# Channel-major weight units: both 512-column products of a k tile ahead of both 256-column ones

## The chip, the cores and the metric

The kernel runs on one NeuronCore of a Trainium2 chip. The metric is the device time of one execution in microseconds, the median of several runs; less is better.

## What is computed

One decoder layer over 256 tokens of width 2048, all in float32. It is a SwiGLU feed-forward half step, then token mixing of two branches side by side (a gated sparse attention of 16 heads and an mLSTM of 4 heads), merged through gates, then a second SwiGLU half step:

```python
def rms_norm(x, gain):
    y = x32 * lax.rsqrt(jnp.mean(x32 * x32, axis=-1, keepdims=True) + EPS)
    return (y * gain).astype(x.dtype)

def swiglu(x, w_gate, w_up, w_down):
    return (jax.nn.silu(x @ w_gate) * (x @ w_up)) @ w_down

x = x + 0.5 * swiglu(rms_norm(x, ffn1_norm), ffn1_w_gate, ffn1_w_up, ffn1_w_down)
hn = rms_norm(x, mix_norm)
proj = hn @ w_in + b_in            # queries, keys, values, gates
...
merged = gates_a * (o_nsa @ w_branch_nsa) + gates_b * (h_m @ w_branch_mlstm)
x = x + merged @ w_out
x = x + 0.5 * swiglu(rms_norm(x, ffn2_norm), ffn2_w_gate, ffn2_w_up, ffn2_w_down)
```

The feed-forward width is 5632. Nearly all of the arithmetic is in the products with the weight matrices, about 408 MB of float32 that are read once.

## The kernel before

Every large product is made in the reduced float32 form of the tensor engine (float32r) from split operands. An activation a is kept as two float32r parts, high and low, side by side: XX, H, M_, O_ and h_ have the shape [128, k tiles, 2, 256 tokens], the index of size 2 being the part. A weight block w is split as it arrives: ACT writes the high part whi as a cast copy of the raw tile (split_hi), DVE writes the low part wlo as the difference (split_lo). The product is then hi·hi + hi·lo + lo·hi.

**The weight stream.** A Unit is a block of a weight matrix that goes through the tensor engine tile by tile. Each tile has 1024 elements per partition (512 KB), is loaded by one DMA on the SP queue into one of 4 raw buffers, and is split into one of 4 whi and one of 4 wlo buffers. The list `plan` holds all tiles in order; the loop at the end of the kernel walks it, and emits the products of each tile in two halves (e = 0 and 1). Between the halves it may start a step of side work (small products of the norms, the attention and the mLSTM), and it issues the split of the tile three places ahead.

There are three kinds of units:

- unit_a, channel-major: the weights are stationary, and the output is [128 columns of w, tokens]. A unit covers 256 columns of w, so a tile holds four k tiles of 128 rows. For each k tile and each block c of 128 columns there are two products: whi against both parts of the activation, 512 columns that move, into the PSUM bank ps[:, c, 0:512], and wlo against the high part alone, 256 columns that move, added into ps[:, c, 0:256]. The function fold adds the two halves of the bank afterwards. All units of the two feed-forward steps are of this kind (but for the last one), and so are the q/k projections of the mLSTM, the merge gates, the two branch outputs and w_out. One narrow unit (w_small, 128 columns) has a single block c.
- unit_b, token-major: the activations are stationary, and the weights move, always 512 columns. Eight or so projections of the mixing stage are of this kind.
- unit_last: the last unit of the second feed-forward step, with three products of 256 columns for each k tile and block.

A guest unit (cmp_unit, the hidden layer of the key and value compression, 256 columns that move) is put between the tiles of a token-major unit. Each product has a weight load of its own ahead of it in the tensor engine's queue. The function mul emits a product of the stream, and behind it a few of the small side products that are waiting, if any (deque small_ones). The class Estimate keeps rough times by which side work is placed; it sums over products, so it is the same for any order of the same products.

In the trace all instructions have the line of one helper, L110, so they are told apart by the tiles: mm<-XX,whi is a product of a channel-major unit with the high part of the weights, mm<-XX,wlo one with the low part, mm<-whi,XX one of a token-major unit.

Of the kernel before, what the change touches and what calls it, by code (L numbers as in the profile page):

```python
# [31 lines left out]

# columns of the packed per-partition vectors
C_G1, C_GM, C_G2 = 0, 16, 32
# [11 lines left out]
class Unit:  # L46
    """A weight matrix block that runs through the tensor engine, tile by tile."""

# [5 lines left out]
class Estimate:  # L54
    """Rough times (us) at which the engines get through what they've been given so far, to tell when a
    piece of side work can go into the tensor engine's queue without holding it up."""
    TABLES = {AF.Exp: 1, AF.Silu: 2, AF.Sigmoid: 3, AF.Gelu_apprx_tanh: 4, AF.Ln: 5}
# [5 lines left out]
    def after(self, t):  # L63
        """What follows on the other engines depends on t, and in turn on itself."""
        self.at, self.by, self.end = t, None, t
# [30 lines left out]
class Engine:  # L96
    """Passes calls on, and counts them in the estimate; or keeps them for later (in kept)."""

# [16 lines left out]
def layer(ctx: ExitStack, tc: tile.TileContext, xt, cols, w_small, b_in,  # L115
# [22 lines left out]
    def side_bank(tag):  # L138
        """A bank for side work; free: the times its two banks are given back."""
        est.q["T"] = max(est.q["T"], free[tag].pop(0))  # L140
        held.append(tag)
        free[tag].append(1e9)
        return aux.tile([128, 512], F32, name=nm(tag), tag=tag, bufs=2)
# [4 lines left out]

    # ------------------------------------------------------------------ persistent tiles
    cl = per.tile([128, NCOL], F32, name="cl")  # L150
# [18 lines left out]

    # ------------------------------------------------------------------ helpers  # L170
    def rsqrt(o, ss, n, inv):
        """o = 1/sqrt(ss*inv + EPS), by Newton steps."""
        v = small(n, tag="rv", bufs=2)[0:o.shape[0]]
        t = small(n, tag="rt", bufs=2)[0:o.shape[0]]
        V.tensor_scalar(v, ss, inv, EPS, op0=OP.mult, op1=OP.add)
        V.tensor_scalar(t.bitcast(I32), v.bitcast(I32), 1, None, op0=OP.logical_shift_right)
        V.tensor_scalar(o.bitcast(I32), t.bitcast(I32), -1.0, float(0x5F3759DF), op0=OP.mult, op1=OP.add)
        for _ in range(3):
            V.scalar_tensor_tensor(t, o, -0.5, o, op0=OP.mult, op1=OP.mult)
            V.tensor_mul(t, t, v)  # L180
            V.scalar_tensor_tensor(o, t, 1.5, o, op0=OP.add, op1=OP.mult)

    cur = {}

    # Side work goes in jobs, and these in steps: products first (up to a yield), then what takes
    # them up (up to a yield, of the names of the jobs that have to be over before it goes on, or of the
    # time from which on it can).
    jobs, past = [], {}
# [27 lines left out]
    def step(forced=None):  # L216
        """Starts a step of a job, if one is due; those without products are done at once."""
        while jobs:
# [30 lines left out]
    def mul(*a, **k):  # L249
        """A product of the weight stream; some small ones of the side work go in behind it."""  # L250
        T.matmul(*a, **k)
        for _ in range(min(len(small_ones), 2 + len(small_ones) % 2)):
            small_ones.popleft()()

    def settle():
        """Takes up the small products that were spread over the last ones of the weight stream."""
        while small_ones:
            small_ones.popleft()()
        j, cur["late"] = cur.get("late"), None
        if j:  # L260
            uptake(j)
# [16 lines left out]

    # ------------------------------------------------------------------ weight stream
    tiles = []  # L280
# [54 lines left out]
    def blocks(w, c0, ncol, kts):  # L335
        """The tiles [128, nk, ncol] of 1024 elements per partition of w[:, c0:c0+ncol]."""
        nk = 1024 // ncol
        v = w.rearrange("(k p) n -> p k n", p=128)
        return [(v[:, k:k + nk, c0:c0 + ncol], nk, ncol) for k in range(0, kts, nk)]

    def unit_b(w, c0, H, L, kts, done, pre=None):
        """Token-major: out[tok, 512 columns], activations stationary."""
        def emit(ps, h, e, wh, wl):
# [9 lines left out]
    def unit_a(w, c0, ncol, kts, act, done, pre=None):  # L353
        """Channel-major: out[128 columns, tok] for each 128 of ncol columns, weights stationary."""
        nk = 1024 // ncol

        def emit(ps, h, e, wh, wl):
            a = act()
            for k in range(e * nk // 2, (e + 1) * nk // 2):
                kt = nk * h + k  # L360
                for c in range(ncol // 128):
                    cs = slice(c * 128, c * 128 + 128)
                    mul(ps[:, c, :], wh[:, k, cs], a[:, kt].rearrange("p a t -> p (a t)"), start=kt == 0, stop=False)
                    mul(ps[:, c, 0:S], wl[:, k, cs], a[:, kt, 0, :], start=False, stop=kt == kts - 1)
        return Unit(blocks(w, c0, ncol, kts), emit, done, pre)

    def unit_last(w, c0, ncol, kts, act, done):
        """As unit_a, but with one sum, and one 128 columns after the other at the end; done(ps, c) for each."""
        nk = 1024 // ncol
# [18 lines left out]
    def fold(o, ps, c=2):  # L388
        """Sum of the two halves that unit_a leaves."""
        A.copy(o, ps[:, 0:c, S:])  # L390
# [3 lines left out]

    # ------------------------------------------------------------------ residual stream pieces

    def g_r():
        """rstd of the residual: R per token, and RB along the free axis on each partition."""
        ps = psS()
# [17 lines left out]
    def residual(pool, c, ps, half, gcol, name):  # L417
        """Adds 256 channels to X; then scales and splits them for the next products."""
        y = pool.tile([128, 2, S], F32, name=nm("y"), tag="y", bufs=2)
# [32 lines left out]

    # ------------------------------------------------------------------ FFN
    def ffn(wg, wu, wd, first, nxt, name):
        """first: the job that leaves this norm's rstd; nxt: the next norm's gain column, or None for
        the last one (then it is stored); name: the job that leaves the next rstd."""
        env = {}
# [61 lines left out]

    # ------------------------------------------------------------------ mixing  # L520
    def mixing():
# [50 lines left out]

        # ---- gate tile: rows 0-3 forget, 32-35 input, 64-111 attention gates
        def gate_done(ps):
# [44 lines left out]

        # ---- compressed keys and values  # L620
        def kcvc_done(ps):
# [6 lines left out]
        def g_flat(kc, w):  # L628
            """The blocks' positions on the partitions, split; columns (part, group, block)."""
            tr = psT().rearrange("p (g t) -> p g t", g=2)  # L630
# [9 lines left out]
            for lp in range(2):  # L640
                o = slice(lp * 64, lp * 64 + 64)
                for gpar in range(2):
                    v = tr[gpar * 64:gpar * 64 + 64, :, lp:]
                    # token 16 * block + 2 * k + lp of group 2 * g + gpar
                    src = bass.AP(tensor=v.tensor, offset=v.offset, ap=[v.ap[0], [2, 16], [S, 2], [16, 15]])
# [70 lines left out]

        # ---- queries and keys, normalised
        def normed(src, dst, n):
            """src, dst [128, 2, 64*n/2]: each 64 columns divided by their rms."""
            yield  # L720
# [39 lines left out]
        def g_qt(q, g):  # L760
            """Of each head of the group, both parts of its queries, one below the other."""
            qs = env["q", g] = env["N"].tile([128, 4, S], F32R, name=nm("qs"), tag="qs", bufs=2)
# [15 lines left out]
        def g_kk(g):  # L778
            """The keys of the group (selected, window), split, each part on both halves of the partitions."""
            kk = env["k", g] = env["N"].tile([128, 2, 2, S], F32R, name=nm("kk"), tag="kk", bufs=2)  # L780
# [23 lines left out]

        # ---- attention
        def gates_of(g):
            """Attention gates of the group: [tok, tile, head, branch]."""
            return env["gat"].rearrange("p t (g r b) -> p t g r b", g=4, r=4)[:, :, g]
# [131 lines left out]

        # ---- mLSTM
        def mv_done(c):
# [149 lines left out]

        # ---- merge
        def sig_done(key, c):
# [103 lines left out]

    # ------------------------------------------------------------------ start
    nc.scalar.dma_start(cl, cols)  # L1200
# [55 lines left out]

    # ------------------------------------------------------------------ run
    banks = {}
# [87 lines left out]
```

## Time and profile before

| | |
|---|---|
| median of 3 runs | 2255.24 us (2254.92 to 2256.05) |
| span of the profiled execution, first to last instruction | 2240.6 us |
| what lies around the span (median less span) | 14.6 us |
| PE busy | 2228.4 us, 99% |
| DVE, ACT busy | 1370.9 us (61%), 1105.6 us (49%) |
| HBM read | 408.40 MB, 183 GB/s over the span |

The span is that of one execution under the profiler; the timed runs are others, and the profiled one has no time of its own but its span. PE is TensorE's products, PEld its weight loads, which overlap the products. The end of a product is modelled by the profiler and overlaps the start of the next; the starts are what is measured. The stages, roughly: the first feed-forward step until 740 us, the token-major projections and the attention until 1020 us, the mLSTM projections and the merge until 1500 us, then the second feed-forward step.

### The profile page before, as it was taken

Reading aid. Unit: us, or ns where it says so; the run is one execution under the profiler, and the core shown is the slowest. Engines: PE = TensorE matmul, PEld = TensorE weight load, DVE = VectorE, ACT = ScalarE, POOL = GpSimd, SP = SyncE. Lnnn points to the kernel's source line nnn. Section 1 sums busy time; section 2 is a strip of 40 time slices with the busy share of each in tenths; the row PEclk is TensorE's granted clock in tenths of the full one; section 3 lists DMA queues with packets and bytes.
Section 4 is the critical chain, followed back from the end, with each engine's and each line's share of the span. In section 5 each row is a group of like instructions: output and inputs, shape, how many; then the busy total and the mean of one; then the engine's idle time right before and its main releaser. Section 6 shows DMA issues by size and latency. Waiting matters only on the chain.

```text
span 2240.6 us, 31889 instructions
## 1 busy us (share of the span) xinstructions
PE 2228.4 (99%) x12685; PEld 1928.6 (86%) x12685; DVE 1370.9 (61%) x1711; ACT 1105.6 (49%) x1471; POOL 27.8 (1%) x54
## 2 busy tenths in 40 slices
PE   9999999999999999999999999999999999999999
PEld 7888888888888888778888888888888888888888
DVE  7656555555555677776766666665555555554553
ACT  6444444444444455566775544554444444443332
POOL 0000000000000000001100000000000000000000
PEclk9999999999999999999999999999999999999999
DMA  7666666666555676444556666655665556565663
GB/s 246 189 190 191 191 188 189 188 188 198 188 189 189 185 238 187 148 123 130 152 163 192 186 187 185 194 182 185 187 186 185 185 185 187 185 195 193 196 196 124
DMA packets 395078, 412.59 MB, mean 184 GB/s; under 512 B 13296, under 2 KB 375920, under 8 KB 394928
## 3 DMA queue, kind: packets, MB, share of 16 engines
q1 hardware_dynamic: 394064, 408.08, 58.9%
q0 software_dynamic: 720, 2.36, 0.4%
q8 instruction: 99, 1.62, 0.3%
q14 instruction: 51, 0.42, 0.1%
q10 hardware_dynamic: 144, 0.11, 0.0%
HBM read 408.40 MB, written 2.10 MB: 183 GB/s over the span
## 4 chain that ended last, share of the span: by engine, by line
PE 97%; DVE 1%; ACT 1%; DMA 1%; issue 0%; SPq 0%; DVEq 0%; ACTq 0%
PE mm L110 94%; PE sc L110 2%; PE tr L110 2%; DVE wlo L110 0%; DMA X<-in_xt_dram 0%; DMA raw<-in_w_in_dram 0%; DVE t L110 0%; DVE nx L110 0%; ACT whi L110 0%; ACT kk L110 0%; ACT t L110 0%; DVE y L110 0%; DVE kk L110 0%; ACT qs L110 0%; ACT XX L110 0%
## 5 line engine op out<-in xcount | busy, mean ns | idle before, releaser
L110 DVE TENSOR_TENSOR wlo<-raw,whi 128x1024 fp32r<-128x1024 f32 (+1 forms) x772 | 929.4, 1224 | 583.4 <-ACT whi L110 580.6
L110 PE MATMUL mm<-XX,whi 128*128 128x512 f32 x3600 | 1269.4, 397 | 4.8 <-DVE XX L110 4.8
L110 ACT CAST whi<-raw 128x1024 fp32r<-128x1024 f32 (+1 forms) x772 | 793.6, 1046 | 581.1 <-PE mm L110 450.1
L110 PE MATMUL mm<-XX,wlo 128*128 128x256 f32 x3600 | 1011.5, 281 | 0.9 <-DVE wlo L110 0.8
L110 PEld LDWEIGHTS mm<-XX,whi 128*128 128x128 f32 x3600 | 676.2, 188 | 165.0 <-ACT whi L110 5.8
L110 PEld LDWEIGHTS mm<-XX,wlo 128*128 128x128 f32 x3600 | 681.2, 189 | 2.7 <-DVE wlo L110 2.5
L110 PE MATMUL mm<-H,whi 128*128 128x512 f32 (+1 forms) x1496 | 493.6, 382 | 0.5 <-DVE y L110 0.5
L110 PE MATMUL mm<-H,wlo 128*128 128x256 f32 x1408 | 395.0, 281 | 0.0
L110 PEld LDWEIGHTS mm<-H,whi 128*128 128x128 f32 x1496 | 274.5, 188 | 58.6 <-DVE y L110 0.7
L110 PEld LDWEIGHTS mm<-H,wlo 128*128 128x128 f32 x1408 | 266.0, 189 | 0.0
L110 PE MATMUL mm<-whi,XX 128*128 128x512 f32 x576 | 192.3, 400 | 0.0
L110 PEld LDWEIGHTS mm<-whi,XX 128*128 128x128 f32 x576 | 108.2, 188 | 21.5 <-issue 0.7
L110 PE MATMUL mm<-wlo,XX 128*128 128x512 f32 x288 | 113.8, 395 | 0.2 <-DVE wlo L110 0.2
L110 PE MATMUL mm<-M__10731,whi 128*128 128x512 f32 x256 | 90.5, 397 | 0.0
L110 PE MATMUL mm<-M__10731,wlo 128*128 128x256 f32 x256 | 71.9, 281 | 0.0
L110 ACT COPY sg<-mm 128x512 f32<-128x512 f32 x44 | 25.8, 587 | 79.8 <-PE mm L110 79.8
L110 ACT COPY sh<-mm 128x512 f32<-128x512 f32 x44 | 25.8, 587 | 78.4 <-PE mm L110 78.4
L110 PEld LDWEIGHTS mm<-wlo,XX 128*128 128x128 f32 x288 | 54.3, 188 | 9.9 <-DVE wlo L110 0.6
L110 DVE TENSOR_TENSOR sg<-mm,sg 128x512 f32<-128x512 f32 x44 | 30.4, 692 | 50.6 <-ACT sg L110 50.5
L110 DVE TENSOR_TENSOR sh<-mm,sh 128x512 f32<-128x512 f32 x44 | 30.4, 692 | 50.2 <-ACT sh L110 50.2
L110 PEld LDWEIGHTS mm<-M__10731,whi 128*128 128x128 f32 x256 | 48.1, 188 | 11.9
L110 ACT CAST H<-sh 128x512 fp32r<-128x512 f32 x44 | 27.3, 621 | 62.1 <-DVE sh L110 62.1
(192 smaller groups left out, 1221.1 us busy)
## 6 DMA issues: line engine op xcount, KB each, us to landing
raw<-in_wu_dram SPq DMA_DIRECT2D x176, 512.0 KB, 4.7
raw<-in_wd_dram SPq DMA_DIRECT2D x176, 512.0 KB, 4.5
raw<-in_wg_dram SPq DMA_DIRECT2D x175, 512.0 KB, 4.7
raw<-in_w_in_dram SPq DMA_DIRECT2D x168, 512.0 KB, 4.4
raw<-in_w_out_dram SPq DMA_DIRECT2D x32, 512.0 KB, 4.5
raw<-in_wb_n_dram SPq DMA_DIRECT2D x16, 512.0 KB, 5.1
raw<-in_wb_m_dram SPq DMA_DIRECT2D x16, 512.0 KB, 4.4
bias<-in_b_in_dram POOLq DMA_DIRECT2D x9, 256.0 KB, 3.7
```

What stands on the lines that cost most here:

```text
L110: return g(out, *a, **k)
```

## The change

In the function emit of unit_a the loop over the blocks c is split in two: first the 512-column products of all blocks of the k tile, then the 256-column products of all blocks. For a unit of 256 columns the order within a k tile becomes whi block 0, whi block 1, wlo block 0, wlo block 1, where it was whi block 0, wlo block 0, whi block 1, wlo block 1. The rest of the diff removes comments and docstrings.

```diff
         def emit(ps, h, e, wh, wl):
             a = act()
             for k in range(e * nk // 2, (e + 1) * nk // 2):
                 kt = nk * h + k
                 for c in range(ncol // 128):
                     cs = slice(c * 128, c * 128 + 128)
                     mul(ps[:, c, :], wh[:, k, cs], a[:, kt].rearrange("p a t -> p (a t)"), start=kt == 0, stop=False)
+                for c in range(ncol // 128):
+                    cs = slice(c * 128, c * 128 + 128)
                     mul(ps[:, c, 0:S], wl[:, k, cs], a[:, kt, 0, :], start=False, stop=kt == kts - 1)
         return Unit(blocks(w, c0, ncol, kts), emit, done, pre)
```

## Rows read from the trace of the kernel before

**Rows 1.** The page's head and the busy time of each engine.

```profile
span 2240.6 us, 31889 instructions
...
PE 2228.4 (99%) x12685; PEld 1928.6 (86%) x12685; DVE 1370.9 (61%) x1711; ACT 1105.6 (49%) x1471; POOL 27.8 (1%) x54
```

**Rows 2.** Groups of PE's products by operands: busy us, mean ns | idle before.

```profile
L110 PE MATMUL mm<-XX,whi 128*128 128x512 f32 x3600 | 1269.4, 397 | 4.8 <-DVE XX L110 4.8
L110 PE MATMUL mm<-XX,wlo 128*128 128x256 f32 x3600 | 1011.5, 281 | 0.9 <-DVE wlo L110 0.8
...
L110 PE MATMUL mm<-H,wlo 128*128 128x256 f32 x1408 | 395.0, 281 | 0.0
...
L110 PE MATMUL mm<-M__10731,wlo 128*128 128x256 f32 x256 | 71.9, 281 | 0.0
...
L110 PE MATMUL mm<-h__9138,wlo 128*128 128x256 f32 x128 | 36.0, 281 | 0.0
L110 PE MATMUL mm<-O__6437,wlo 128*128 128x256 f32 x128 | 36.0, 281 | 0.0
```

**Rows 3.** Busy time of each engine by stretch, then clock and DMA.

```profile
core 0: us, PE busy (x) PEld busy (x) DVE busy (x) ACT busy (x) POOL busy (x), PEclk, DMA share, GB/s
...
14.00:44.00 30.00, 29.87 (x172) 25.77 (x170) 24.19 (x31) 21.47 (x32) 0.00 (x0) 1.00 0.82 262
45.00:740.00 695.00, 695.00 (x4013) 612.87 (x4012) 402.68 (x411) 319.40 (x365) 0.00 (x0) 1.00 0.61 190
...
1020.00:1183.00 163.00, 162.51 (x942) 141.70 (x938) 113.23 (x214) 114.21 (x174) 16.56 (x21) 1.00 0.54 158
1183.00:2205.00 1022.00, 1022.00 (x5795) 886.87 (x5794) 596.30 (x614) 470.32 (x550) 0.00 (x0) 1.00 0.61 189
```

**Rows 4.** Timeline of PE in FFN1: start us, busy us, product.

```profile
300.30 0.39 PE L110 MATMUL mm<-XX,whi 128*128 128x512 f32 x1
300.53 0.28 PE L110 MATMUL mm<-XX,wlo 128*128 128x256 f32 x1
300.65 0.39 PE L110 MATMUL mm<-XX,whi 128*128 128x512 f32 x1
```

**Rows 5.** Timeline of the weight loads in the same stretch.

```profile
300.30 0.19 PEld L110 LDWEIGHTS mm<-XX,wlo 128*128 128x128 f32 x1
300.53 0.19 PEld L110 LDWEIGHTS mm<-XX,whi 128*128 128x128 f32 x1
```

**Rows 6.** Timeline of PE in FFN2.

```profile
2000.05 0.40 PE L110 MATMUL mm<-H,whi 128*128 128x512 f32 x1
2000.29 0.28 PE L110 MATMUL mm<-H,wlo 128*128 128x256 f32 x1
2000.40 0.40 PE L110 MATMUL mm<-H,whi 128*128 128x512 f32 x1
...
2001.11 0.40 PE L110 MATMUL mm<-H,whi 128*128 128x512 f32 x1
```

**Rows 7.** Timeline of PE in a token-major unit; nine products lie between these starts.

```profile
799.71 0.39 PE L110 MATMUL mm<-wlo,XX 128*128 128x512 f32 x1
...
801.75 0.39 PE L110 MATMUL mm<-wlo,XX 128*128 128x512 f32 x1
```

**Rows 8.** Timeline of PE at the guest block's start and end (16 products).

```profile
803.56 0.28 PE L110 MATMUL sc<-whi,flat 128*128 128x256 f32 x1
803.67 0.28 PE L110 MATMUL sc<-wlo,flat 128*128 128x256 f32 x1
...
805.47 0.40 PE L110 MATMUL mm<-whi,XX 128*128 128x512 f32 x1
805.71 0.40 PE L110 MATMUL mm<-wlo,XX 128*128 128x512 f32 x1
805.94 0.62 PE L110 MATMUL mm<-whi,XX 128*128 128x512 f32 x2
```

**Rows 9.** Timeline of PE: small side products within the stream of FFN1.

```profile
43.90 0.50 PE L110 MATMUL sc<-ones,acc 128*128 128x2 f32 x4
```

## The prediction

> **What bounds the kernel now.** I read the page first. The span is 2240.6 us and PE is busy for 99% of it [rows 1], so no other engine can matter except by making PE wait. The groups of products by operand come next: the pairs of the channel-major units (a 512-column product with whi, a 256-column one with wlo) are 3600 + 1408 + 256 + 128 + 128 products of 256 columns, less 88 of unit_last, so 5432 pairs; PE idles 4.8 us ahead of the 512s, once, at the start, and 0.9 us ahead of the 256s [rows 2]. Nothing is waited for in the body. What is left to change is the pace at which products follow each other, and a busy time can't show that, because the products overlap in it (0.39 us busy, the next one 0.23 us later [rows 4]). So I went to starts.
>
> The table of stretches is the first thing to look at [rows 3]: the granted clock is 1.00 in all of them, PE has no gap, and yet the paces differ. From 45 to 740 us, 4013 products in 695 us make 2005 pairs at 0.347 us. From 1183 to 2205 us, 5795 products, all but 12 in pairs, make 2891 pairs at 0.3535 us. The timeline of single products says the same: 300.30 to 300.65 is 0.35 for one pair, split 0.23 and 0.12 [rows 4]; and 2000.05 to 2001.11 is 1.06 for three pairs, 0.3533 each [rows 6]. So the same code runs at two paces, A (346.7 ns) and B (353.3 ns), 6.7 ns apart. B is not FFN2's own: the first 44 us of FFN1 have it too, and there it ends right behind a group of small side products at 43.90 [rows 9]. I take the pace for a state in which the stream settles after a disturbance and which it then keeps. In B the 256 still takes 0.11 to 0.12 us (2000.29 to 2000.40); the 6.7 ns lie on the 512 (0.24 at 2000.05) [rows 6].
>
> How much there is to win: pairs at B are some 2891 after 1183 us, some 95 in the first 45 us, and about half of the 416 between 1020 and 1183 us, where side work keeps disturbing it (my choice; that half is worth 1.4 us) [rows 3]. That is some 3190 pairs x 6.67 ns = 21.3 us above pace A, 0.9% of the time.
>
> **The change part by part.** Per k tile of 256 columns the order 512, 256, 512, 256 becomes 512, 512, 256, 256. No instruction is added or removed; the 16 pairs of the gate unit (128 columns, one block) keep their order, so 5416 pairs are 2708 k tiles that change. DMAs, splits, folds and PSUM banks are the same.
>
> *What moves for the other engines.* wlo is first read one 512-product later, 0.23 us: that can win at most the 0.9 us of idle time ahead of wlo products [rows 2]; I take 0.3. The last read of a whi tile starts one 256-product (0.12 us) sooner, which hands the buffer back to ACT sooner; PE doesn't wait for ACT anywhere in [rows 2], so it is worth 0; without the cover of the four buffers it would be a gain too. The last product of a unit is the same one, so the folds start as before. Side products that follow each product of the stream now stand behind other products, in the same number.
>
> *What moves on PE: the sequence of sizes.* Each product has its own weight load, which starts with the product before it: loads start at 300.30 and 300.53, as the products do, and show 0.19 us [rows 5]. Before, each k tile had two loads beside 512s and two beside 256s; after, also two and two. So a load finds as much cover as before, only in another order. The new neighbours are 512 behind 512 and 256 behind 256. The trace has both. In the token-major units, 512s alone: 799.71 to 801.75 is 2.04 for nine products, 227 ns each [rows 7]. 256s alone, in the guest block of the compression unit: 803.67 to 805.47 is 1.80 for fifteen, 120 ns each [rows 8]. Two of each are 693 ns, which is pace A again (2 x 346.7). So equal neighbours cost nothing over A, and A cannot be beaten by them: that is the lower bound, 693 ns for a k tile, against 707 in B.
>
> What the crossing from one size to the other costs is shown at the ends of the same block. The first 256 behind the 512s takes 0.11 (803.56 to 803.67), the first 512 behind the 256s 0.24 (805.47 to 805.71) and the second 0.23 [rows 8]. With a second 256 at 0.12 that is 0.24 + 0.23 + 0.11 + 0.12 = 0.70 us for one round trip of two and two, 7 ns over the 693. B has the same 7 ns for a round trip of one and one. So the reading I choose: the 6.67 ns of B are paid once per round trip from 256 to 512 and back, and the change halves the round trips. In A they are not paid, and 693 stays 693.
>
> The sum, with states as they are now: 3190 pairs are 1595 k tiles; one price in place of two saves 1595 x 6.67 ns = 10.6 us. With the 0.3 us for wlo, 10.9 us. The 14.6 us between span and median (2255.24) are untouched. 2255.24 - 10.9 = 2244.3 us, or -0.48%; the profiled execution's span would go from 2240.6 to 2229.7. Bounds: all k tiles at 693 saves the 21.3 us; all at 707 (the price paid twice in each) adds 6.67 ns x the 5432 - 3190 = 2242 pairs now at A, 15.0 us; the 0.70 us read at the block's ends, taken for every k tile, is 350 ns a pair against a mean of 346.7 + 21.3 us / 5432 = 350.6 now, next to no change.
>
> *A rule against a row.* The row: a 512 that another 512 follows takes 227 ns, a 256 that a 256 follows 120 ns, each some 13 ns over its columns at 2.4 GHz [rows 7, 8]. The Trainium skill (TensorE: Matmul & The Clock Gate, Back-to-back issue gap) gives a product's distance to the next as its columns at the clock plus some 2.5 ns, whatever stands beside it. By that a k tile is 650 ns in either order and the change would do nothing; the trace does not agree with the 650, and its two paces speak against a price that knows no neighbour.
>
> **The rivals.**
>
> *All slow: the crossing is paid with two products.* At the guest block's end not one but two 512s are long, 0.24 and 0.23 (805.47 to 805.94 is 0.47 for the two, against 0.454 for two of 227), because the stream needs more than one product to settle [rows 8]. In a k tile of two and two it never settles: both 512s carry the excess, as each 512 of B does (353 less 117 for its 256, so 236), and the 256s are at 117 and 120. Then a k tile is 2 x 236 + 237 = 709 ns or so, B's pace, and, worse, the stretch that runs at A now (45 to 740 us) has no calm state left to fall into. Price: the 15.0 us above, 2270 us, +0.66%; if a fall into A remains in a third of the time, 2263. It decides from 702 ns a k tile on, which is today's mean (2 x 350.6). For it: the two long 512s. Against: 512s alone do settle, at 227 [rows 7], and the sum of the four at the block's ends is 0.70, not 0.71. Chance 0.29.
>
> *Nothing measurable: all at 700.* The crossing's 7 ns are paid once in every k tile, in the stretch that is at A today too, because two different sizes in a row of four never fall into step. Then the 10.9 us won in B are given back by the 1000 k tiles of A x 6.67 ns = 6.7 us and 0.7 us in the mixed stretch: -3.5 us, 2251.7 us, -0.15%. The skill's rule above ends beside it, at 2255. For it: the block's ends, read as they stand, give 0.70 without saying which state they are in. Against: A exists, at 346.7, for a sequence that changes size at each product. Chance 0.20, the case without any effect included.
>
> *All calm: A everywhere.* Equal neighbours let the stream settle as 512s alone do [rows 7], and B is gone: -21.3 - 0.3 us, 2233.6 us, -0.96%. For it: 512s alone and 256s alone settle to 227 and 120 and I see no B among them. Against: only two of each are in a row. Chance 0.16.
>
> **How the numbers follow.** The forecast (states as now, the price once for a k tile) has 0.35, with its own range of 2240 to 2249, since a state that is drawn anew behind each disturbance moves a stretch from one pace to the other. A run that differs by 0.2% (4.5 us) can be told from no change here. Faster by over 0.2%: 0.35 x 0.95 + 0.16 + a few hundredths of the 0.20 = 0.51. Within 0.2%: 0.22. Slower: 0.27, the all-slow rival less its mildest form. The range leaves one in ten at either end: from 2232, just under all calm, to 2267, in the all-slow case.
>
> **What would show it.** Right: in the timeline of the FFN stretches the starts go 0.23, 0.23, 0.12, 0.12; the k tile is 0.693 or 0.700 us; in FFN2 the pairs' count over the window gives 350 ns or less for a pair; the count of instructions, the clock and the waits are as before. Wrong: the second 512 is as long as the first, 0.235 or more, and the pair in 100 to 740 us is over 347 ns. The forecast would also be wrong if the state of the long stretches is drawn otherwise: FFN1 at the slow pace or FFN2 at the calm one is worth 6.7 or 9.6 us each.

## The result and the profile after

The changed kernel takes 2229.36 us (median of 4 runs, 2229.07 to 2229.7), the kernel before 2255.08 us (4 runs, 2254.64 to 2256.05). The ratio is 0.9892, with a 95% interval of 0.9873 to 0.991: 1.1% faster. The forecast was 2244.3 us with a range of 2232 to 2267. The sign was right; the time lies below the range, and the gain is 25.7 us where 10.9 were forecast. All four runs of the kernel before are of one kind here; the section on e1 shows that it has two times, and that the gain is 25.7 us over the longer one only.

The span tells a second story. It went from 2240.6 to 2227.3 us, 13.3 us less, while the time went 25.7 us down. What lies around the span was 14.6 us before and is 2.1 us after (2229.36 - 2227.3). No product of the change lies outside the span, so one of the two numbers of before did not belong to the other. That is what the first experiments are about.

The stretches of the changed kernel, with the columns of [rows 3]:

```profile
core 0: us, PE busy (x) PEld busy (x) DVE busy (x) ACT busy (x) POOL busy (x), PEclk, DMA share, GB/s
45.00:740.00 695.00, 695.00 (x3993) 606.48 (x3992) 401.29 (x407) 318.31 (x364) 0.00 (x0) 1.00 0.61 189
1020.00:1183.00 163.00, 162.67 (x951) 141.68 (x950) 112.11 (x213) 114.86 (x177) 16.60 (x21) 1.00 0.54 156
1183.00:2195.00 1012.00, 1012.00 (x5829) 884.23 (x5828) 600.75 (x620) 472.36 (x552) 0.00 (x0) 1.00 0.61 191
```

Compare the counts. Between 45 and 740 us the changed kernel gets through 3993 products, the profiled execution of before through 4013 [rows 3]: here the new order is the slower one, by 0.5%. Behind 1183 us it makes 5829 products in 1012 us, 5.76 a us, against 5.67 before, 1.6% more. The clock is 1.00 in all three, as before.

PE's groups of products, with the columns of [rows 2]:

```profile
L110 PE MATMUL mm<-XX,whi 128*128 128x512 f32 x3600 | 1136.5, 397 | 5.6 <-DVE XX L110 4.7 <-ACT whi L110 0.8
L110 PE MATMUL mm<-XX,wlo 128*128 128x256 f32 x3600 | 709.8, 278 | 0.8 <-DVE wlo L110 0.8
L110 PE MATMUL mm<-H,wlo 128*128 128x256 f32 x1408 | 284.2, 278 | 0.0
```

The idle time is nearly what it was: 5.6 and 0.8 us, against 4.8 and 0.9 [rows 2]. The 0.8 us more are one wait for a whi tile of ACT, at 10.62 us, while the stream starts up; the prediction had put nothing there. The busy time of the groups fell by far more than the span (709.8 against 1011.5 us for the 256s), but only because two products of one group that stand side by side overlap in it; that column says nothing about the pace. The starts do. The timeline of the same stretch of FFN2 as in [rows 6], products of one kind merged:

```profile
2000.16 0.63 PE L110 MATMUL mm<-H,whi 128*128 128x512 f32 x2
2000.62 0.39 PE L110 MATMUL mm<-H,wlo 128*128 128x256 f32 x2
2000.85 0.63 PE L110 MATMUL mm<-H,whi 128*128 128x512 f32 x2
2001.32 0.40 PE L110 MATMUL mm<-H,wlo 128*128 128x256 f32 x2
2001.55 0.63 PE L110 MATMUL mm<-H,whi 128*128 128x512 f32 x2
2002.02 0.39 PE L110 MATMUL mm<-H,wlo 128*128 128x256 f32 x2
2002.25 0.62 PE L110 MATMUL mm<-H,whi 128*128 128x512 f32 x2
```

From 2000.16 to 2002.25 are 2.09 us for three k tiles: 697 ns each. The two 512s take 0.46 to 0.47 of it, the two 256s 0.23 to 0.24. In FFN1 it is the same (3676 products from 100 to 740 us, 919 k tiles, 696 ns each). So the k tile is at 697 ns everywhere, 348.3 a pair: neither the 693 of pace A nor the 707 of pace B, and the same in the stretch that was at A and in the one that was at B.

### The profile page after: what moved, and what is told of

It is laid out like the page before. It is cut to its first block, busy times and chain, and to the rows that moved or that the text cites. A ratio compares the mean times of both kernels' runs of the same rounds, so it can differ in the third digit from the quotient of the medians.

```text
span 2227.3 us, 31889 instructions
## 1 busy us (share of the span) xinstructions
PE 2214.6 (99%) x12685; PEld 1916.3 (86%) x12685; DVE 1370.8 (62%) x1711; ACT 1105.2 (50%) x1471; POOL 27.8 (1%) x54
## 4 chain that ended last, share of the span: by engine, by line
PE 97%; DVE 1%; ACT 1%; DMA 0%; issue 0%; SPq 0%; DVEq 0%; ACTq 0%
PE mm L110 94%; PE sc L110 2%; PE tr L110 2%; DVE wlo L110 0%; DMA raw<-in_wu_dram 0%; DMA raw<-in_w_in_dram 0%; DVE t L110 0%; DVE nx L110 0%; ACT whi L110 0%; ACT kk L110 0%; ACT t L110 0%; DVE y L110 0%; DVE kk L110 0%; ACT qs L110 0%; SPq L295 0%
## 5 line engine op out<-in xcount | busy, mean ns | idle before, releaser
L110 PE MATMUL mm<-XX,whi 128*128 128x512 f32 x3600 | 1136.5, 397 | 5.6 <-DVE XX L110 4.7
L110 PE MATMUL mm<-XX,wlo 128*128 128x256 f32 x3600 | 709.8, 278 | 0.8 <-DVE wlo L110 0.8
L110 PEld LDWEIGHTS mm<-XX,whi 128*128 128x128 f32 x3600 | 550.1, 189 | 7.3 <-ACT whi L110 6.0
L110 PE MATMUL mm<-H,whi 128*128 128x512 f32 (+1 forms) x1496 | 446.4, 382 | 0.5 <-DVE y L110 0.5
L110 PE MATMUL mm<-H,wlo 128*128 128x256 f32 x1408 | 284.2, 278 | 0.0
L110 PEld LDWEIGHTS mm<-H,whi 128*128 128x128 f32 x1496 | 228.4, 189 | 0.7 <-DVE y L110 0.7
L110 PE MATMUL mm<-M__10731,whi 128*128 128x512 f32 x256 | 79.9, 393 | 0.0
L110 ACT ACTIVATE sg<-sg 128x512 f32<-128x512 f32 x44 | 27.8, 632 | 60.2 <-DVE sg L110 60.2
L110 PEld LDWEIGHTS mm<-M__10731,wlo 128*128 128x128 f32 x256 | 48.1, 188 | 10.9
```

Of the source, the lines that this page charges most:

```text
L110: return g(out, *a, **k)
```

## The experiments

### Which pace does a timed execution have?

**e1 and e8: the kernel before, unchanged.**

> The kernel before, unchanged, profiled once more. Theory 1 (drawn state: which of the two paces the long stretch of FFN1 has is drawn in each execution, and the timed executions run at the slow pace, 353.3 ns a pair, all through): time 2255; the span is either 2240 to 2241 again (the profiled execution draws the calm pace between 45 and 740 us) or some 2253 (it doesn't). Theory 2 (timed and profiled executions have the same paces, and the 14.6 us between span and time lie around the span): span 2240.6, time 2255.

> The kernel before, unchanged, profiled a third time. Theory 1: span 2240 to 2241 or some 2253, as the pace of FFN1 is drawn. Theory 2: 2240.6.

e1 was 2255.7 us in the median, but its 8 runs are not one group: six lie between 2254.97 and 2257.18, two at 2241.94 and 2242.55. The 34 runs of the kernel before that were made beside it do the same: 11 between 2241.96 and 2244.16, 23 between 2254.33 and 2257.21, and none in between (the intervals of the ratios below are as wide as they are because of these two groups). With the two sets made beside the later experiments, 28 of 74 runs lie in the short group. Both new profiled executions had the long time (2257.18 and 2254.58 us), with spans of 2255.5 and 2252.9 us, so that 1.7 us lie around the span in both. By the same 1.7 us the execution that the prediction read (span 2240.6) took 2242.3, in the short group. The table of stretches of e1, products and clock:

```profile
core 0: us, PE busy (x), PEclk, DMA share, GB/s
14.00:44.00 30.00, 30.00 (x169) 1.00 0.79 244
100.00:740.00 640.00, 640.00 (x3624) 1.00 0.60 186
1200.00:1400.00 200.00, 200.00 (x1135) 1.00 0.64 190
1600.00:2190.00 590.00, 590.00 (x3341) 1.00 0.60 189
```

From 100 to 740 us there are 3624 products, 1812 pairs at 353.2 ns. The execution that the prediction was made from had the pace A of 346.7 there. In the merge and in FFN2 the two executions agree (1135 products from 1200 to 1400 us, 3341 from 1600 to 2190 us in both). So the kernel before has two times, 2242 and 2255, some 13 us apart, by the pace of FFN1 (2005 pairs x 6.67 ns = 13.4 us); the profile read for the prediction was of the one, the median of the other. Over the short group the change wins 13 us, over the long one 25.7.

Where the two part can be read in the traces. First the execution of the prediction:

```profile
44.69 0.39 PE L110 MATMUL mm<-XX,whi 128*128 128x512 f32 x1
...
49.55 0.40 PE L110 MATMUL mm<-XX,whi 128*128 128x512 f32 x1
49.78 0.60 PE L110 MATMUL sc<-dg,ones 128*128 128x128 f32 x4
...
50.70 0.39 PE L110 MATMUL mm<-XX,whi 128*128 128x512 f32 x1
...
52.43 0.39 PE L110 MATMUL mm<-XX,whi 128*128 128x512 f32 x1
```

and e1:

```profile
46.20 0.40 PE L110 MATMUL mm<-XX,whi 128*128 128x512 f32 x1
...
51.05 0.40 PE L110 MATMUL mm<-XX,whi 128*128 128x512 f32 x1
51.29 0.61 PE L110 MATMUL sc<-dg,ones 128*128 128x128 f32 x4
...
52.20 0.40 PE L110 MATMUL mm<-XX,whi 128*128 128x512 f32 x1
...
53.97 0.40 PE L110 MATMUL mm<-XX,whi 128*128 128x512 f32 x1
```

Ahead of the group of side products (sc<-dg,ones) both are at pace A (14 pairs in 4.86 and in 4.85 us). Behind the same group, the first stays at A (five pairs in 1.73 us, 346 ns) and e1 goes over to B (five in 1.77, 354), and each keeps its pace to the end of FFN1. The first 44 us had the other order of paces: B in the execution of the prediction, A in e1 and e8 (82 pairs from 16.18 to 44.61 us in e1, 346.7 ns each). So one and the same disturbance can leave either pace; what decides which was not found.

**e2 and e3: the new order in one part alone.** In both, the two orders stand in the function emit and the weight matrix chooses:

```diff
-                for c in range(ncol // 128):
-                    ... (whi product of c, wlo product of c)
+                n = range(ncol // 128)
+                for f, c in [(f, c) for f in (hi, lo) for c in n] if any(w is v for v in (wg1, wu1, wd1)) else [(f, c) for c in n for f in (hi, lo)]:
+                    f(c)
```

with `not any(...)` in e3.

> The new order in the units of the first feed-forward step alone (1056 k tiles). Theory 1: the timed runs go there from 353.3 to 348.3 ns a pair, 1056 x 10 ns = 10.6 us less, 2244.5. Theory 2: the stretch goes from the calm 346.7 to 348.3, 1002 x 3.3 ns = 3.3 us more, 2258.5. Span of the profiled execution in both: about 2244 (FFN1 at 348.3, FFN2 at 353.3).

> The new order in all channel-major units but those of the first feed-forward step (1652 k tiles). Theory 1: what e2 leaves of the whole gain of 25.7 us, 15 us less, 2240. Theory 2: 29 us less, 2226. Span of the profiled execution: some 2224 if it draws the calm pace in FFN1, some 2237 if not.

e2: 2244.97 us, all 12 runs between 2244.42 and 2247.29, ratio 0.9973 (0.9954 to 0.9991); theory 1 said 2244.5, theory 2 2258.5. With the new order in FFN1 there is one group of times only. e3: 2238.88 us in the median of 11 runs, ratio 0.9921 (0.9895 to 0.9946), with six runs between 2238.88 and 2240.36 and five between 2226.03 and 2227.39; theory 1 said 2240. Both groups are there, since FFN1 still has the old order, and each is 15 to 16 us under the group of before that answers to it. Over the long group of before (2255.68 in the median), e2 saves 10.7 us and the long group of e3 15.7 us, together 26.4, near the 25.7 of the whole change. Theory 2 is refuted by the spans of e1 and e8 and by e2; the short group of e3 alone would fit it too, because FFN1 is calm there.

**e4 and e12: a kick.** Four (e12: one) tiny products go ahead of the seventh unit of FFN1, in the old order:

```diff
+        if u is units[6] and i == 0:
+            for _ in range(4):
+                T.matmul(ps[:, 0, 0:2], ident, ones[:, 0:2], start=True, stop=True)
         for e in range(2):
             u.emit(ps, i, e, wh, wl)
```

> The kernel before with four tiny products (two columns each, into a bank that the next product starts afresh) ahead of the seventh unit of the first feed-forward step. By themselves they cost about 0.5 us. Theory 1: they draw the pace of the rest of FFN1 anew (about 620 us, 1790 pairs): 2255.5 if the slow one comes again, 2243.5 if the calm one does (1790 x 6.67 ns = 11.9 us less). Theory 2: FFN1 is calm already: 2255.5 or, if the slow pace is drawn, 2267.

> As e4 with one tiny product in place of four. If any short disturbance sets the calm pace: 2243.5. If it depends on the disturbance's length which pace is drawn: 2255, or now the one and now the other.

e4: 2243.98 us, all 10 runs between 2243.22 and 2246.04, ratio 0.9968 (0.9948 to 0.9988). Four tiny products that compute nothing make the kernel before 11 us faster. The timeline around them (each tiny product is two records; one wlo product lies behind each whi product):

```profile
89.06 0.40 PE L110 MATMUL mm<-XX,whi 128*128 128x512 f32 x1
...
90.48 0.40 PE L110 MATMUL mm<-XX,whi 128*128 128x512 f32 x1
...
90.83 0.95 PE L110 MATMUL mm<-ones,ident 128*128 128x2 f32 x8
91.64 0.48 PE L110 MATMUL mm<-XX,whi 128*128 128x512 f32 x1
...
92.42 0.39 PE L110 MATMUL mm<-XX,whi 128*128 128x512 f32 x1
...
93.81 0.39 PE L110 MATMUL mm<-XX,whi 128*128 128x512 f32 x1
```

Ahead of the kick, 89.06 to 90.48 is 1.42 us for four pairs, 355 ns; behind it, 92.42 to 93.81 is 1.39 for four, 347 ns, and it stays so: 3695 products from 100 to 740 us, as in the calm execution of before (3694), where e1 has 3624. From 90.48 to 92.42 are three pairs and the kick, 1.94 us; less 1.06 for the pairs, the kick itself costs 0.88 us, not the 0.5 expected. The products on both sides of it are of the same kinds in the same order, and e1 kept the slow pace through the same ones; so the pace is a state that the stream is in, and not fixed by its data, its buffers or the stage.

With one tiny product (e12) the median is 2249.67 us, and the runs fall into both groups again: five of ten between 2241.63 and 2243.67, five between 2255.66 and 2256.36. That can't be told from no kick at all (28 of 74). In e12's profiled execution FFN1 was calm ahead of the one product (110 pairs from 50.34 to 88.48 us, 346.7 ns each) and stayed so. Why four set the calm pace here and one doesn't was not found.

**e9: the same kick in the changed kernel.**

> The changed kernel with the same four tiny products as in e4. Theory 1 (the new order has one pace, 696.7 ns for a k tile, whatever disturbs it): 2229.4 + 0.5 = 2230, and 696.7 ns ahead of the kick and behind it. Rival (the new order has two paces too, and 693 can be drawn): 2227 or lower.

2230.26 us (four runs, 2229.84 to 2230.58), 0.9 us over the changed kernel: the kick's own cost, 0.88 us in e4, and nothing else. Behind the kick the profile has 3677 products from 100 to 740 us, where the changed kernel has 3676. In every trace with the new order (the changed kernel, e2, e3, e9, e11) the stretches that have it show this one pace, and the disturbance tried here does not move it.

### Is it the order of sizes, or the banks?

The new order changes two things together: which size follows which, and whether a product adds into the PSUM bank that the one before it wrote. e5 and e6 take them apart.

```diff
+                # e5
+                for f, c in ((hi, 0), (lo, 0), (lo, 1), (hi, 1)) if ncol == 256 and 0 < kt < kts - 1 else ...:
+                # e6
+                for f, c in ((hi, 0), (lo, 1), (hi, 1), (lo, 0)) if ncol == 256 and 0 < kt < kts - 1 else ...:
```

> Order within a k tile: 512 of block 0, 256 of block 0, 256 of block 1, 512 of block 1 (first and last k tile of a unit as in the changed kernel). The sizes follow each other as in the changed kernel (two 512s, two 256s, round and round), but each 256 of block 0 again stands right behind the 512 that writes its PSUM bank, and the two 512s in a row have different k tiles. Theory of sizes (the order of sizes alone sets the pace): 348.3 ns a pair, 2229 to 2231. Rival, banks (the change wins because neighbours write different PSUM banks or share the moving activation): half or none of the gain, 2242 to 2255.

> Order within a k tile: 512 of block 0, 256 of block 1, 512 of block 1, 256 of block 0 (first and last k tile of a unit as in the kernel before). Sizes alternate as before; but no 256 stands right behind the 512 of its own PSUM bank. Theory of sizes: two paces, 346.7 or 353.3 ns a pair, no gain at 2255, or 2242 if a calm FFN1 is drawn. Rival, banks: 2229 to 2242.

e5, sizes as in the changed kernel, banks nearly as before: 2231.24 us, ratio 0.9911 (0.9881 to 0.9941). The timeline of e5:

```profile
300.14 0.62 PE L110 MATMUL mm<-XX,whi 128*128 128x512 f32 x2
300.60 0.40 PE L110 MATMUL mm<-XX,wlo 128*128 128x256 f32 x2
300.83 0.63 PE L110 MATMUL mm<-XX,whi 128*128 128x512 f32 x2
301.30 0.39 PE L110 MATMUL mm<-XX,wlo 128*128 128x256 f32 x2
301.53 0.85 PE L110 MATMUL mm<-XX,whi 128*128 128x512 f32 x3
```

Two k tiles in 300.14 to 301.53 are 695 ns each within the rounding, and 3676 products fall between 100 and 740 us, the changed kernel's number. Of the 2 us more only a part can stand where each unit's first and last k tile break the cycle (the three 512s at 301.53): in the profiled executions e5 is 2.1 us behind the changed kernel after the first 100 products of the stream (28.56 against 26.44 us) and 3.6 us behind at its last one (2227.01 against 2223.38), so 1.5 us come in over the rest. That the breaks cost these was not shown. e6, sizes as before, no 256 behind its own 512: 2254.75 us in the median, ratio 1.0005 (0.998 to 1.003), and both groups again (three of ten at 2241.62 to 2242.14). So the order of sizes makes the gain, and the banks make none of it; nor does the moving activation that the two 512s share in the changed kernel, for in e5 they don't share it. The two 256s share theirs in both, which no run takes apart.

### Is more of the same better?

**e7: four 512s, then four 256s** (both k tiles of a half tile together).

```diff
+            kk = [(k, nk * h + k) for k in range(e * nk // 2, (e + 1) * nk // 2)]
+            for k, kt in kk:
+                ... (whi products of both blocks)
+            for k, kt in kk:
+                ... (wlo products of both blocks)
```

> Both k tiles of a half tile together: four 512s, then four 256s. Theory a (each round trip from 512 to 256 and back costs 3.3 ns, the excess of 696.7 over 693.3, whatever its length): 695 ns for a k tile, 4.5 us under the changed kernel, 2225. Theory b (the ends of the guest block: the first four 512s behind 256s take 234, 235, 229, 232, the first four 256s 113, 119, 120, 120): 701 ns for a k tile, 12 us over the changed kernel, 2241.

2240.06 us (12 runs, 2239.66 to 2241.95), ratio 0.9958 (0.9938 to 0.9978): faster than before, but 10.7 us over the changed kernel. The timeline of e7:

```profile
300.39 0.63 PE L110 MATMUL mm<-XX,wlo 128*128 128x256 f32 x4
300.86 1.09 PE L110 MATMUL mm<-XX,whi 128*128 128x512 f32 x4
301.79 0.64 PE L110 MATMUL mm<-XX,wlo 128*128 128x256 f32 x4
302.26 1.09 PE L110 MATMUL mm<-XX,whi 128*128 128x512 f32 x4
```

Four 512s take 0.93 (300.86 to 301.79), four 256s 0.47: 1.40 us for two k tiles, 700 each. Theory b, read from the ends of the guest block [rows 8], said 701. A fixed price per round trip (theory a) is refuted, and the traces show by place where the time goes. On the mean over 100 to 740 us, the next start lies 234, 235, 232 and 228 ns behind e7's four 512s, and 118, 120, 119 and 118 behind its four 256s. In the changed kernel it is 233 and 233, then 115 and 116. So a longer run of 512s comes down to the 227 of 512s alone [rows 7] only at its fourth, and a longer run of 256s loses the shortness of the first two.

### A version that beats both

A calm old order (346.7 ns a pair) is better than the new one (348.3), if it can be had reliably. e10 keeps the old order and kicks at four places; e11 has the old order with a kick in each feed-forward step, and the new order in the mixing stage, where side work disturbs the stream all the time.

```diff
+        if any(u is units[n] for n in (6, -48)) and i == 0:   # e10: (6, -85, -60, -48)
+            for _ in range(4):
+                T.matmul(ps[:, 0, 0:2], ident, ones[:, 0:2], start=True, stop=True)
```

> The kernel before (old order) with the four tiny products at four places: the seventh unit of the first feed-forward step, the unit behind the first mLSTM branch unit, the first unit of w_out, the fifth unit of the second feed-forward step. If a kick always sets the calm pace, as in e4, FFN1 is 346.7 from 92 us on and FFN2 from 1545 us on (some 1870 pairs): 2244 - 12.5 + 1.5 = 2233, and up to 5 us less if the merge keeps the calm pace too. If each kick draws anew: 2233 to 2246, the same kernel differing from run to run.

> Old order in both feed-forward steps with a kick in each (as in e10), new order in the channel-major units of the mixing stage (620 k tiles). With both steps calm: 2244 - 12 for FFN2 + 0.5 - 620 x 10 ns = 2226, some 3 us under the changed kernel. If the kick in FFN2 draws the slow pace: 2238.

e10: 2234.01 us (2233.33 to 2235.64), ratio 0.993 (0.9904 to 0.9956). The kick in FFN2 made it calm (3405 products from 1600 to 2190 us against 3341 in e1). Those of the merge did not: 1136 products from 1200 to 1400 us, as in e1, and the first of the two leaves the slow pace from its first pairs on:

```profile
1189.76 0.95 PE L110 MATMUL mm<-ones,ident 128*128 128x2 f32 x8
...
1191.00 0.40 PE L110 MATMUL mm<-XX,whi 128*128 128x512 f32 x1
...
1192.06 0.40 PE L110 MATMUL mm<-XX,whi 128*128 128x512 f32 x1
```

That is 1.06 us for three pairs, and from 1191.00 to 1399.40 us 590 pairs take 353.2 ns each. So a kick of four doesn't always set the calm pace. In FFN1 it sets it and does not merely change it over: in the profiled executions of e10 and e11 FFN1 was calm ahead of the kick and stayed so, where in e4 it was slow ahead.

e11: 2226.16 us (6 runs, 2225.22 to 2227.76), ratio 0.9894 (0.9868 to 0.9921), 3.2 us under the changed kernel, which was not run beside it; e9, which was, is the changed kernel with a kick, and its lowest run is 2229.84. (The 620 k tiles of its expectation are 640: 2708 less 1056 in FFN1 and 1012 in FFN2, which is worth 0.2 us.) The stretches of e11:

```profile
100.00:740.00 640.00, 640.00 (x3694) 1.00 0.61 190
1200.00:1400.00 200.00, 200.00 (x1152) 1.00 0.63 189
1600.00:2190.00 590.00, 590.00 (x3410) 1.00 0.61 192
```

3694 and 3410 products in the feed-forward stretches are pace A (in the second the 256s of unit_last begin just before its end), 1152 in the merge that of the new order (1135 in the old one).

## Why the prediction was wrong, point by point

*What bounds the kernel:* right. PE sets the time, and what changes is the distance between its starts. No wait of more than 0.8 us (the one for ACT at the start), no DMA and no other engine had a part.

*Two paces, and a state that a disturbance draws:* right for the old order, and shown by e1 and e4. That the new order would have two paces as well, by the state before it, was not so (e9).

*"The sum, with states as they are now":* this step failed first. It took the paces of the one profiled execution for those of the timed runs, and the 14.6 us between span and median, called untouched, hid the contradiction: 12 to 13 us of those 14.6 were pace B in FFN1, which the median had and the profile had not. With B in nearly all of it, e2 and e3 show what the timed runs won: 10.7 us in FFN1, where the forecast had next to nothing, and 15.7 in the rest, where it had nearly all of its 10.9. The prediction named a state drawn otherwise as a sign of being wrong, but took the kernel before to be as its one profile has it. It also held 0.2% to be enough to tell a change from none, and had its chances by that; the kernel before differs from itself by 0.6%.

*"693 stays 693", and "the 6.67 ns of B are paid once per round trip":* this failed too. A k tile of the new order is 697 ns in both, so where B was it saves 10 ns and not 6.67, and where A was it costs 3.3. The 512s are where B's price lay, as the prediction said: on the mean 230 ns at A (100 to 740 us of the profile that it read), 236 at B (1600 to 2190 us), with 117 for the 256s at either. In the new order the price is not gone from one 512 and left on the other: both take 233, and the 256s 115 and 116. Redone with both: 2708 k tiles x 10 ns = 27.1 us, less 13.3 ns for some 104 k tiles that are calm in the disturbed stretch of 1020 to 1183 us, 1.4 us: 25.7 us, the measured gain. The 104 is the prediction's half, not a count, so that this comes out to the tenth is luck. For the profiled pair the same numbers give -14.5 us (1446 k tiles behind 1183 us) + 3.3 us (1002 k tiles in FFN1) - 0.5 us (the first 45 us) - 0.7 us (the disturbed stretch, half of its 208 k tiles at A, half at B): -12.4 us, against the 13.3 by which the spans differ. That the forecast of the span (2229.7 for 2227.3) came so near was luck too: a k tile behind 1183 us won more than forecast, and FFN1, left at nothing, lost.

*The 0.3 us for wlo:* not seen; the idle time ahead of wlo products of XX is 0.8 us for 0.9.

*The rivals.* All calm had nearly the right time (2233.6) for a wrong reason: no k tile settles at 693, but there were more slow pairs to win from than the profile showed. All slow did not come, though both 512s of a k tile are long: 233 ns each where it put 236, and 115 and 116 for the 256s where it put 117 and 120. All at 700 has the right shape, one price in every k tile, with 700 for 697; it too was summed from the wrong execution.

The price that knows no neighbour, which the prediction took from the Trainium skill (TensorE: Matmul & The Clock Gate, Back-to-back issue gap), would have left the time as it was. That section gives it for an isolated product, and says that in a stream of weight loads and products both set the spacing; the prediction left this out, and no run here tests it. The traces do not agree with the price, with 707 and 697 ns for the same four products in two orders.

## What to carry to other kernels

When the time around the profiled span is large for a kernel of that kind (14.6 us here, 2.1 after), compare the single runs, more than a few of them, before using the profile's numbers for the median: a kernel can have two times, the profile shows one of them, and four runs can all be of the other. For a stream of products, measure the pace as products per stretch from the starts; busy time and idle time show nothing of it. And an order that keeps one pace through all disturbances can be worth more than one whose best pace is a little better but only sometimes drawn.

## What the runs showed of the hardware that was not expected

Products of reduced float32, each with its own weight load, alternating 512 and 256 columns, run at 346.7 or at 353.3 ns a pair on one and the same chip, at a granted clock of 1.00, and keep either for hundreds of microseconds. A few small products in between can set which: with four tiny ones in FFN1 the calm pace came in all 22 runs (e4, e10, e11), with none in 28 of 74, and with one in 5 of 10, which is no different from none. In the merge four did not set it (e10). The order 512, 512, 256, 256 has one pace in all its traces (348.3 a pair), four and four has 350.6 (3651 products from 100 to 740 us). Both lie over the 346.7 that 227 and 120 for either size alone give [rows 7, 8], though they have more equal neighbours than the alternation that reaches it. What in the tensor engine or its reads makes the stream lock in this way stays open; no run here separates the two.
